# Output projection of a hybrid decoder layer: another order of its 32 products, split weight tiles shared between token quarters, and the MLP's first operands made in two rounds

## The chip, the cores and the metric

One core of one Trainium2 chip runs the whole layer in one launch. The metric is the device time of one execution in microseconds (us).

## The reference

One decoder layer, all in float32, for 2048 tokens of width 1024. The change touches the point where the two groups of mixer heads end and the MLP begins:

```python
mix = concatenate([gdn_out, hgrn_out])          # 2048 x 1024
y   = mix @ w_out                                # output projection, 1024 x 1024
h1  = x + rms_norm(y, post_mix_norm)             # norm over the 1024 columns of a token
t   = rms_norm(h1, pre_mlp_norm)
u   = relu(t @ w_mlp_up) ** 2                    # 1024 x 4096
m   = u @ w_mlp_down
```

Behind it the residual, a norm and a gated input embedding follow; they are not touched.

## The kernel before

**Layout.** Activations stand transposed: a tile is 128 features on the partitions by 512 tokens. The 2048 tokens are four quarters `q` of 512 (`NQ`), the 1024 features eight blocks of 128 (`KD`). A product of the projection, `mmo_q_d`, gives feature block `d` of quarter `q`; it accumulates over the eight blocks `k` of the mixed heads.

**Split operands.** A float32 operand is split into a high and a low part (`split`, L160 ff.): ACT copies it rounded (L164), DVE subtracts (L165). A product of two split operands takes three matmuls, so one `mmo` is 8 x 3 = 24 matmuls. A split weight tile of `w_out` (`whl`, 1 MB, three buffers) serves all k of one d. It is made from a raw tile of 512 KB (`raw`, two buffers, `stage_out`, load L338). `split_in_place` does the same to the mixed heads `mixT`, which `mix_operands(q)` loads (the tiles live in a ring of 28 buffers that also takes the MLP's operands).

**Order.** The 32 products run in the list `order`: all eight d of quarter 0, then 1, 2, 3. I call the places in this list slots, 0 to 31. Slots 0 and 1 are computed earlier, while the previous stage ends (`held`). At slot j the program makes the split tile of slot j + 2 ready (`ready_out`) and loads the raw tile of slot j + 3 (`stage_out`). Quarters 0, 1 and 2 load raw tiles and split them anew, 24 times; in quarter 0 the split tile is also stored to memory (`keep`, `cache_out`, 1 MB each), and quarter 3 reloads it from there (`reload`, L185).

**Agenda.** Work beside the products is written as generators. `later(gen, offsets)` sets their steps on a clock that ticks once in eight matmuls of PE (`mm`, `tick`); a step's instructions are then put into the queues at that place. Each engine, and SP as the queue for most DMAs, runs its instructions in that order.

- After each product: ACT copies the result out of PSUM (L1392, `yo`), ACT and DVE add its square to a sum (`squares`, L233 and L234). Quarters 2 and 3 store `yo` to memory (`yod`).
- Norm of a quarter after its last product (`rstd_steps`): the sum is split (`hl_o`), two matmuls with ones on PE spread it over partitions (`nrm_o`, L1174 and L1175), then ACT (Ln, Exp, Square) and DVE make the reciprocal root `r_o`.
- Quarters 0 and 1 go on in `normed`, `residual_by_dma`: for each d DVE scales `yo` (L1228), POOL issues a DMA that adds x from memory onto it (L1229); five steps later its square is added (`sq_h`, `acc_h`) and SP stores it as `h1d` (L1232). The sum of these squares is split (`hl_h`) and goes through PE as `nrm_h`, which gives the second norm's root `rn`. The steps stand in `OUT_STEPS`: 1 for `hl_o`, 5 for `nrm_o`, 7 to 19 for the residual, 20 for `hl_h`, 26 for `nrm_h`.
- Quarters 2 and 3 store a row of `r_o`; their residual comes later.
- MLP operands of the first half (quarters 0 and 1): the up product uses seven combinations of tiles per k (`11, 3, 1, 2, 21, 4, 22`). `early_operands` makes the ones that need quarter 0 alone (`11` and `21`: load `be`, multiply, split), from slot 17 on; `up_operands(0, ...)` the five others, `run(early)` first, from the slot after the second quarter's `nrm_h`, for each k all five in turn.
- In the last slots the raw tiles of the first up weights are loaded (`u_raw`) and split (`w_u`). Then the first MLP group runs (`u`, also L1143), with the fourth quarter's `nrm_o` among its matmuls.

Of the kernel before, what the change touches and what calls it, by code (L numbers as in the profile page):

```python
# [20 lines left out]
P = 128  # L21
# [22 lines left out]
N_CONST = C_MASK + len(LEVELS)  # L44


OUT_STEPS = (1, 5) + tuple(range(7, 20)) + (20, 26)
MLP_STEPS = (1, 5) + tuple(range(7, 25, 2))
AMID_STEPS = (1, 5) + tuple(range(12, 39, 3))

# [38 lines left out]
def trunk(ctx, tc, x, xT, pT, vecs, w_in, w_ab, gdn_a_log, gdn_dt_bias, w_out, w_up, w_down,  # L89
# [19 lines left out]
    def blk(c):  # L109
        return slice(c * P, (c + 1) * P)  # L110
# [51 lines left out]
    def split(t, eng, raw):  # L162

        S.activation(t[:, 0], raw, AF.Copy)  # L164
        eng.tensor_tensor(t[:, 1], raw, t[:, 0], ALU.subtract)  # L165
# [11 lines left out]
    def keep(key, w):  # L177

        c = dr.tile([P, 2 * KD * P], F32, name=f"cache_{key}")
        nc.sync.dma_start(c, w.bitcast(F32).rearrange("p h k n -> p (h k n)"))  # L180
        cached[key] = c

    def reload(key, name):
        w = wp.tile([P, 2, KD, P], F32R, tag="whl", name=f"w_{name}")
        nc.sync.dma_start(w.bitcast(F32).rearrange("p h k n -> p (h k n)"), cached[key])  # L185
        return w
# [142 lines left out]
            xin[q].append(t)  # L329
            yield  # L330

    order = [(q, d) for q in range(NQ) for d in range(KD)]
    staged_out, ready, RAW = {}, {}, 3

    def stage_out(j):
        if j < len(order) and order[j][0] < RAW:
            raw = wp.tile([P, KD, P], F32, tag="raw", name=f"raw_out{j}", bufs=2)
            nc.sync.dma_start(raw, w_out[order[j][1]])  # L338
            staged_out[j] = raw

    def ready_out(j):
        if j >= len(order):
            return
        if j not in staged_out:
            ready[j] = reload(f"out{order[j][1]}", f"out{j}")
            return
        ready[j] = wp.tile([P, 2, KD, P], F32R, tag="whl", name=f"w_out{j}")
        split(ready[j], V, staged_out.pop(j))
        if order[j][0] == 0:
            keep(f"out{order[j][1]}", ready[j])  # L350

    clock, agenda = [0], {}

# [927 lines left out]
    def early_operands():  # L1281

        start_operands(0)
        for k in range(KD // 2):
            for n, kk in (("11", k), ("21", k + KD // 2)):
# [3 lines left out]
                moving(0, n, k, b)  # L1289
                yield  # L1290

    def up_operands(half, rsb):

        qs = (2 * half, 2 * half + 1)
        early = half in tops
        if not early:
            start_operands(half)
        for k in range(KD // 2):
            n = f"{half}_{k}"
            b11, b21, b12, b22, t3, t2, t4 = (once(lambda i=i: ytile(f"b{i}_{n}")) for i in range(7))  # L1300
            if early:
                b11, b21 = (lambda k=k: first_b[k]), (lambda k=k: first_b[k + KD // 2])
            for b, s, kk in ((b12, 1, k), (b22, 1, k + KD // 2), (b11, 0, k), (b21, 0, k + KD // 2)):
                if early and s == 0:
                    continue
# [3 lines left out]
            if not early:  # L1309
                moving(half, "11", k, b11())  # L1310
# [8 lines left out]
            if not early:  # L1319
                moving(half, "21", k, b21())  # L1320
# [30 lines left out]
        return halves[1]  # L1351

    pair[0] = True
    for j, (q, d) in enumerate(order):
        if d == 0:
            ys, acc = [], None
            if q < 2:
                later(mix_operands(q + 1), range(2, 18, 2))
            if q == 1:
                later(mix_operands(3), range(17, 25))  # L1360
        ready_out(j + 2)
        stage_out(j + 3)
        if j == len(order) - 5:
            u_raw = [wp.tile([P, 2, QT], F32, tag="raw", name=f"u_raw{i}", bufs=2) for i in range(2)]
            a1, a2 = w_up[0], w_up[FF // P // 2]
            for t, i, src in ((u_raw[0], 0, a1[:, : KD // 2]), (u_raw[1], 1, a1[:, KD // 2 :]),
                              (u_raw[0], 1, a2[:, : KD // 2]), (u_raw[1], 0, a2[:, KD // 2 :])):
                nc.sync.dma_start(t[:, i].rearrange("p (k n) -> p k n", n=P), src)
        if j == len(order) - 2:
            two_blocks(("11", u_raw[0][:, 0]), ("12", u_raw[1][:, 1]))  # L1370
        if j == len(order) - 1:
            (a11, a21), (s1, s4) = ((t[:, 0], t[:, 1]) for t in u_raw)
            b22 = two_blocks(("22", s1), None)
            V.tensor_tensor(s1, s1, a21, ALU.add)
            V.tensor_tensor(a21, a11, a21, ALU.subtract)
            V.tensor_tensor(a11, s1, a11, ALU.subtract)
            V.tensor_tensor(s4, s4, a11, ALU.subtract)
            u_block("3", b22, a21)
        if (q, d) == (2, 1):
            early = early_operands()  # L1380
            later(early, range(0, 2 * KD, 2))
        if prep is None and h1_r[1] is not None:
            run(early)
            prep = up_operands(0, h1_r)
            later(prep, range(0, 24, 1))
        if j in held:
            ps = held.pop(j)
        else:
            ps = bank(f"mmo_{q}_{d}", pp)
            product(ps, columns(ready.pop(j)), xin[q])  # L1390
        y = ytile(f"yo{q}_{d}") if q < 2 else tp.tile([P, QT], F32, tag="stg", name=f"yo{q}_{d}")
        S.activation(y, ps, AF.Copy)  # L1392
# [439 lines left out]
```

## Time and profile before

| | us |
|---|---|
| three runs: median (lowest to highest) | 2725.19 (2724.35 to 2733.05) |
| profiled execution: span | 2719.9 |
| PE busy in it | 2660.8 (98%) |
| DVE busy | 2040.8 (75%) |
| ACT busy | 1464.0 (54%) |
| POOL busy | 118.5 (4%) |
| slots 2 to 31 of the projection | 1127.46 to 1313.90 |
| first MLP group | 1313.90 to 1335.43 |

The profiled execution has no time of its own beside its span; the span is 5.3 us under the median of the runs, and a change of the span is set against that median. PE's busy time says little about its rate, since matmuls overlap: a matmul's record lasts about 0.39 us, while in an undisturbed run one starts every 0.227 us. So the pitch, the gaps and the granted clock are what to look at. In the rows of the profile buffer numbers are left out: `w_out`, `yo`, `t` stand for all tiles of that name.

### The profile page before, as it was taken

The numbers are of one execution on the slowest core, as the hardware profiler recorded it, in microseconds if no ns is written. First come the engines' busy times: TensorE is split into PE (matmuls) and PEld (weight loads), VectorE is DVE, ScalarE is ACT, GpSimd is POOL, SyncE is SP. The second block draws the span as 40 slices with busy tenths as digits, with TensorE's granted clock in tenths as the row PEclk, the third lists the DMA queues.
The fourth block names the chain that finished last, engine by engine and source line by source line (L and its number), as shares of the span: only waits on it lengthen the run. The fifth ranks groups of instructions, "written<-read, shape, count | busy, mean of one in ns | idle before, by whom it ended". The sixth has DMA issues, their size and how long they took to land.

```text
span 2719.9 us, 38475 instructions
## 1 busy us (share of the span) xinstructions
PE 2660.8 (98%) x12745; PEld 2215.1 (81%) x12745; DVE 2040.8 (75%) x4219; ACT 1464.0 (54%) x2940; POOL 118.5 (4%) x133
## 2 busy tenths in 40 slices
PE   8999999999999999998999999999999999999999
PEld 6788888888888887876788888888888888888887
DVE  7778878787777777576989867768787765567776
ACT  7665555465445455575655646555555545465432
POOL 0000000000000000011000000001000000001000
PEclk9999999999999999998999999999999999999999
DMA  8777777667666665887566457667454346577663
GB/s 282 273 237 255 236 263 242 216 214 241 213 201 221 223 213 164 271 281 231 177 232 228 175 178 240 216 202 244 164 196 163 139 172 207 193 256 247 216 212 131
DMA packets 268742, 589.24 MB, mean 217 GB/s; under 512 B 55658, under 2 KB 60232, under 8 KB 249344
## 3 DMA queue, kind: packets, MB, share of 16 engines
q1 hardware_dynamic: 266240, 582.59, 63.9%
q0 software_dynamic: 2304, 4.20, 0.9%
q8 instruction: 101, 1.65, 0.3%
q14 instruction: 97, 0.79, 0.1%
HBM read 419.75 MB, written 166.92 MB: 216 GB/s over the span
## 4 chain that ended last, share of the span: by engine, by line
PE 51%; DMA 3%; DVE 3%; issue 3%; ACT 1%; POOL 1%; SPq 0%; POOLq 0%; DVEq 0%; ACTq 0%
PE d L1143 22%; PE u L1143 22%; PE mmg L1143 6%; PE mmo L1143 1%; DMA raw_out<-in_w_out_dram 1%; DMA yo<-in_xT_dram 0%; PE mme L191 0%; POOL acc_y L234 0%; DMA b<-h1d 0%; DMA w_out<-cache_out 0%; DMA db<-hid 0%; DVE t L165 0%; DMA h1d<-yo 0%; POOL yo L1229 0%; DVE pr_g L698 0%
## 5 line engine op out<-in xcount | busy, mean ns | idle before, releaser
L1072 PE MATMUL mm<-xt,w 128*128 128x512 f32 x3072 | 784.1, 400 | 1.4 <-ACT zt_zg L577 1.1
L1072 PEld LDWEIGHTS mm<-xt,w 128*128 128x128 f32 x3072 | 553.3, 189 | 102.3 <-ACT zt_zg L577 1.5
L1143 PE MATMUL d<-db,da 128*128 128x512 f32 x2688 | 611.0, 389 | 0.5 <-ACT db L217 0.2
L1143 PE MATMUL u<-t,wu 128*128 128x512 f32 x2604 | 591.1, 389 | 0.0
L1143 PEld LDWEIGHTS d<-db,da 128*128 128x128 f32 x2688 | 504.3, 188 | 106.4 <-DVE db L218 1.0
L1143 PEld LDWEIGHTS u<-t,wu 128*128 128x128 f32 x2604 | 488.7, 188 | 101.5
L218 DVE TENSOR_TENSOR db<-db 128x512 fp32r<-128x512 f32 x224 | 159.9, 714 | 72.4 <-ACT db L217 71.7
L1495 DVE TENSOR_TENSOR u<-u,u 128x512 f32<-128x512 f32 x224 | 150.2, 681 | 58.1 <-PE u L1143 56.6
L1143 PE MATMUL mmo<-mixT,w_out 128*128 128x512 f32 x720 | 173.4, 402 | 11.8 <-DMA w_out<-cache_out 5.5
L217 ACT ACTIVATE db<-db 128x512 fp32r<-128x512 f32 x224 | 140.9, 629 | 78.2 <-DMA db<-hid 71.9
L1143 PEld LDWEIGHTS mmo<-mixT,w_out 128*128 128x128 f32 x720 | 139.5, 195 | 44.6 <-DMA w_out<-cache_out 5.9
L1143 PE MATMUL mmg<-h2T,wg 128*128 128x512 f32 (+1 forms) x792 | 174.8, 383 | 0.0
L1538 ACT ACTIVATE u<-u 128x512 f32<-128x512 f32 x128 | 80.8, 631 | 166.3 <-DVE u L1495 166.0
L1143 PEld LDWEIGHTS mmg<-h2T,wg 128*128 128x128 f32 x792 | 145.5, 188 | 29.1
L165 DVE TENSOR_TENSOR da<-da 128x512 fp32r<-128x512 f32 x128 | 93.7, 732 | 77.7 <-ACT da L164 77.1
L164 ACT ACTIVATE da<-da 128x512 fp32r<-128x512 f32 x128 | 80.5, 629 | 124.8 <-DMA da<-sumd 91.6
L164 ACT ACTIVATE wu<-a 128x512 fp32r<-128x512 f32 x124 | 75.0, 623 | 44.3 <-DMA a<-in_w_up_dram 43.0
L698 DVE TENSOR_TENSOR pr_g<-xs_g,sys_g 128x16 f32<-128x16 f32 (+14 forms) x240 | 94.4, 393 | 5.6
L165 DVE TENSOR_TENSOR wu<-a,wu 128x512 fp32r<-128x512 f32 x124 | 85.6, 693 | 10.8 <-ACT wu L164 10.5
L234 POOL TENSOR_TENSOR acc_y<-acc_y,sq_y 128x512 f32<-128x512 f32 x28 | 38.5, 1374 | 1261.6 <-ACT sq_y L233 1260.8
L1539 ACT ACTIVATE u<-u 128x512 f32<-128x512 f32 x128 | 80.5, 629 | 3.1
L165 DVE TENSOR_TENSOR da<-dr,da 128x512 fp32r<-128x512 f32 x96 | 66.3, 691 | 19.0 <-ACT da L164 16.5
(385 smaller groups left out, 3792.6 us busy)
## 6 DMA issues: line engine op xcount, KB each, us to landing
w<-cache_in SPq DMA_DIRECT2D x96, 1024.0 KB
db<-hid SPq DMA_DIRECT2D x224, 256.0 KB
cache_in<-w SPq DMA_DIRECT2D x32, 1024.0 KB
hid<-u SPq DMA_DIRECT2D x128, 256.0 KB
da<-sumd SPq DMA_DIRECT2D x128, 256.0 KB
a<-in_w_up_dram SPq DMA_DIRECT2D x124, 256.0 KB
hid<-ht SPq DMA_DIRECT2D x96, 256.0 KB
dr<-in_w_down_dram SPq DMA_DIRECT2D x96, 256.0 KB
```

What stands on the lines that cost most here:

```text
L164: S.activation(t[:, 0], raw, AF.Copy)
L165: eng.tensor_tensor(t[:, 1], raw, t[:, 0], ALU.subtract)
L217: S.activation(t[:, 0], plain(t), AF.Copy)
L218: V.tensor_tensor(t[:, 1], plain(t), t[:, 0], ALU.subtract)
L234: eng.tensor_tensor(acc, acc, sq, ALU.add)
L698: V.tensor_tensor(pr[:, :, :, 0:i], xs[:, None, :, 0:i].broadcast_to([P, 2, GC, i]), sys[:, 0:i, i : i + 2].rearrange("p j two -> p two j" ...
L1072: PE.matmul(ps, *terms[i], start=i == 0, stop=i == nt - 1)
L1143: PE.matmul(ps, a, b, start=start, stop=stop)
L1495: V.tensor_tensor(c[new], c[old], ps, ALU.add)
L1538: S.activation(c[k], c[k], AF.Relu)
L1539: S.activation(c[k], c[k], AF.Square)
```

## The change

- `OUT_ORDER` lists the slots as quarter and block: quarter 0 as before, then quarter 1 from block 7 back, then quarters 2 and 3 mixed. A split tile stays for up to three slots that use the same block, if it is among those of the last six slots (`SHARE`). 19 tiles are loaded and split; none is stored or reloaded.
- `ready_at(n)`: tile n is split at the slot after the third last tile in use was used for the last time (three buffers); `stage_at(n)`: its raw tile is loaded one slot after tile n - 2 was split (two buffers). The order gives these slots (load: slot of the load, slot of the split, slots that use it):

```
 5: 2, 3: 5 10      6: 3, 4: 6 9       7: 4, 5: 7 8       8: 5, 9: 11
 9: 6,10: 12       10: 10,11: 13      11: 11,12: 14 16 18  12: 12,13: 15 17 20
13: 13,14: 19 22   14: 14,19: 21 24   15: 15,21: 23 25   16: 20,23: 26 29
17: 22,25: 27 30   18: 24,26: 28 31
```

- The mixed heads of all later quarters are set on the agenda at slot 0.
- The second quarter's steps are `OUT_LAST`: `nrm_o` at 4, residual from 5 to 17, `hl_h` at 19, `nrm_h` at 23.
- `rest_operands` replaces `up_operands` for the first half: round one makes tiles 3 and 4 of each k, round two tiles 2, 1 and 22 of each k from what round one kept. It starts at slot 24 (was 25).
- The third quarter's norm follows slot 28; the fourth's steps are 12, 20 and 24, so that its `nrm_o` falls into the second MLP group.

```diff
--- before.py
+++ after.py
@@ -44,7 +44,10 @@
 N_CONST = C_MASK + len(LEVELS)
 
 
+OUT_ORDER = ("00 01 02 03 04 05 06 07 17 16 15 12 13 14 10 11 20 21 30 22 31 23 32 24 33 34 25 26 27 35 36 37")
+SHARE = 6
 OUT_STEPS = (1, 5) + tuple(range(7, 20)) + (20, 26)
+OUT_LAST = (1, 4) + tuple(range(5, 18)) + (19, 23)
 MLP_STEPS = (1, 5) + tuple(range(7, 25, 2))
 AMID_STEPS = (1, 5) + tuple(range(12, 39, 3))
 
@@ -329,25 +332,31 @@
             xin[q].append(t)
             yield
 
-    order = [(q, d) for q in range(NQ) for d in range(KD)]
-    staged_out, ready, RAW = {}, {}, 3
-
-    def stage_out(j):
-        if j < len(order) and order[j][0] < RAW:
-            raw = wp.tile([P, KD, P], F32, tag="raw", name=f"raw_out{j}", bufs=2)
-            nc.sync.dma_start(raw, w_out[order[j][1]])
-            staged_out[j] = raw
-
-    def ready_out(j):
-        if j >= len(order):
-            return
-        if j not in staged_out:
-            ready[j] = reload(f"out{order[j][1]}", f"out{j}")
-            return
-        ready[j] = wp.tile([P, 2, KD, P], F32R, tag="whl", name=f"w_out{j}")
-        split(ready[j], V, staged_out.pop(j))
-        if order[j][0] == 0:
-            keep(f"out{order[j][1]}", ready[j])
+    order = [(int(s[0]), int(s[1])) for s in OUT_ORDER.split()]
+    load_of, last_use, tile_of = [], [], []
+    for j, (q, d) in enumerate(order):
+        recent = [n for n in range(len(tile_of)) if tile_of[n] == d and n in load_of[-SHARE:]]
+        if not recent:
+            recent = [len(tile_of)]
+            tile_of.append(d)
+            last_use.append(j)
+        load_of.append(recent[0])
+        last_use[recent[0]] = j
+    staged_out, ready = {}, {}
+
+    def ready_at(n):
+        return 0 if n < 3 else sorted(last_use[:n])[n - 3] + 1
+
+    def stage_at(n):
+        return 0 if n < 4 else ready_at(n - 2) + 1
+
+    def stage_out(n):
+        staged_out[n] = wp.tile([P, KD, P], F32, tag="raw", name=f"raw_out{n}", bufs=2)
+        nc.sync.dma_start(staged_out[n], w_out[tile_of[n]])
+
+    def ready_out(n):
+        ready[n] = wp.tile([P, 2, KD, P], F32R, tag="whl", name=f"w_out{n}")
+        split(ready[n], V, staged_out.pop(n))
 
     clock, agenda = [0], {}
 
@@ -1289,25 +1298,44 @@
                 moving(0, n, k, b)
                 yield
 
+    def rest_operands(rsb):
+
+        held = []
+        for k in range(KD // 2):
+            b11, b21 = first_b[k], first_b[k + KD // 2]
+            b12, b22 = ytile(f"b2_0_{k}"), ytile(f"b3_0_{k}")
+            for b, kk in ((b12, k), (b22, k + KD // 2)):
+                nc.sync.dma_start(b, h1d[1][kk])
+                V.scalar_tensor_tensor(b, b, col(R_PREMLP + kk), rsb, ALU.mult, ALU.mult)
+            yield
+            t3 = ytile(f"b4_0_{k}")
+            V.tensor_tensor(t3, b22, b12, ALU.subtract)
+            V.tensor_tensor(b12, b12, b11, ALU.subtract)
+            moving(0, "3", k, t3)
+            yield
+            t2, t4 = ytile(f"b5_0_{k}"), ytile(f"b6_0_{k}")
+            V.tensor_tensor(t2, b22, b12, ALU.subtract)
+            V.tensor_tensor(t4, b21, t2, ALU.subtract)
+            moving(0, "4", k, t4)
+            held.append((t2, b12, b22))
+            yield
+        for k, raws in enumerate(held):
+            for n, raw in zip(("2", "1", "22"), raws):
+                moving(0, n, k, raw)
+                yield
+
 ...
@@ -1351,15 +1378,19 @@
         return halves[1]
 
     pair[0] = True
+    early = None
+    made, square_sums = {q: [None] * KD for q in range(NQ)}, {q: None for q in range(NQ)}
     for j, (q, d) in enumerate(order):
-        if d == 0:
-            ys, acc = [], None
-            if q < 2:
-                later(mix_operands(q + 1), range(2, 18, 2))
-            if q == 1:
-                later(mix_operands(3), range(17, 25))
-        ready_out(j + 2)
-        stage_out(j + 3)
+        if j == 0:
+            later(mix_operands(1), range(2, 18, 2))
+            later(mix_operands(2), range(20, 36, 2))
+            later(mix_operands(3), range(35, 43))
+        for n in range(2, len(tile_of)):
+            if ready_at(n) == j:
+                ready_out(n)
+        for n in range(3, len(tile_of)):
+            if stage_at(n) == j:
+                stage_out(n)
         if j == len(order) - 5:
             u_raw = [wp.tile([P, 2, QT], F32, tag="raw", name=f"u_raw{i}", bufs=2) for i in range(2)]
             a1, a2 = w_up[0], w_up[FF // P // 2]
@@ -1376,28 +1407,31 @@
             V.tensor_tensor(a11, s1, a11, ALU.subtract)
             V.tensor_tensor(s4, s4, a11, ALU.subtract)
             u_block("3", b22, a21)
-        if (q, d) == (2, 1):
+            later(prep, range(3 * KD // 2))
+        if early is None and h1_r[0] is not None:
             early = early_operands()
             later(early, range(0, 2 * KD, 2))
         if prep is None and h1_r[1] is not None:
             run(early)
-            prep = up_operands(0, h1_r)
-            later(prep, range(0, 24, 1))
+            prep = rest_operands(h1_r[1])
+            later(prep, range(3 * KD // 2))
         if j in held:
             ps = held.pop(j)
         else:
             ps = bank(f"mmo_{q}_{d}", pp)
-            product(ps, columns(ready.pop(j)), xin[q])
+            product(ps, columns(ready[load_of[j]]), xin[q])
         y = ytile(f"yo{q}_{d}") if q < 2 else tp.tile([P, QT], F32, tag="stg", name=f"yo{q}_{d}")
         S.activation(y, ps, AF.Copy)
-        acc = squares(acc, ps, d, f"o{q}")
-        ys.append(y)
+        acc = square_sums[q] = squares(square_sums[q], ps, d, f"o{q}")
+        made[q][d] = y
         if q >= 2:
             nc.sync.dma_start(yod[q][d], y)
-        if d == KD - 1 and q < 2:
-            later(normed(q, ys, acc, lambda d, q=q: xT[blk(d), tok(q)], R_POSTMIX, h1d[q], "o", "h"), OUT_STEPS)
-        elif d == KD - 1:
-            later(rstd_steps(acc, 1.0 / D, EPS, f"o{q}", row_of(o_r, q), po, wait=True), OUT_STEPS[:2] + (9,))
+        if all(of != q for of, _ in order[j + 1 :]) and q < 2:
+            later(normed(q, made[q], acc, lambda d, q=q: xT[blk(d), tok(q)], R_POSTMIX, h1d[q], "o", "h"),
+                  OUT_LAST if q else OUT_STEPS)
+        elif all(of != q for of, _ in order[j + 1 :]):
+            later(rstd_steps(acc, 1.0 / D, EPS, f"o{q}", row_of(o_r, q), po, wait=True),
+                  OUT_STEPS[:2] + (9,) if q == 2 else (12, 20, 24))
     u_block("2", two_blocks(("1", s1), None), a11)
     u_block("4", wp.tile([P, 2, KD // 2, P], F32R, tag="raw", name="w_u4", bufs=2), s4)
     run(prep)
```

More of the change, by code (lines that the diff above doesn't have):

```diff
@@ L1290, in early_operands @@
                 yield
+    def rest_operands(rsb):
[22 more added lines that the diff above has]
+                yield
     def up_operands(half, rsb):
         qs = (2 * half, 2 * half + 1)
-        early = half in tops
-        if not early:
-            start_operands(half)
+        start_operands(half)
         for k in range(KD // 2):
@@ L1300, in up_operands @@
             b11, b21, b12, b22, t3, t2, t4 = (once(lambda i=i: ytile(f"b{i}_{n}")) for i in range(7))
-            if early:
-                b11, b21 = (lambda k=k: first_b[k]), (lambda k=k: first_b[k + KD // 2])
             for b, s, kk in ((b12, 1, k), (b22, 1, k + KD // 2), (b11, 0, k), (b21, 0, k + KD // 2)):
-                if early and s == 0:
-                    continue
                 nc.sync.dma_start(b(), h1d[qs[s]][kk])
@@ L1308, in up_operands @@
             yield
-            if not early:
-                moving(half, "11", k, b11())
+            moving(half, "11", k, b11())
             V.tensor_tensor(t3(), b22(), b12(), ALU.subtract)
@@ L1318, in up_operands @@
             moving(half, "2", k, t2())
-            if not early:
-                moving(half, "21", k, b21())
+            moving(half, "21", k, b21())
             yield
```

## Prediction

> **What bounds the kernel now.** TensorE is busy for almost the whole span, so the question is only where it is not at its pitch in the stage that the change rewrites: output projection and first group of the MLP's up product. I cut that stretch into windows. The columns are window and length, then busy time (instructions) of PE, PEld, DVE, ACT and POOL, the granted clock, the DMA share and GB/s; the first row is the whole stretch, the others are parts of it.
>
> ```profile
> 1127.46:1335.43 207.97, 195.07 (x817) 157.34 (x816) 144.44 (x215) 127.51 (x201) 16.33 (x18) 0.96 0.75 241
> 1127.46:1173.58 46.12, 43.75 (x186) 35.47 (x184) 22.48 (x30) 23.96 (x38) 2.01 (x2) 0.96 0.86 298
> 1232.49:1272.93 40.44, 31.57 (x110) 24.40 (x111) 25.55 (x38) 16.63 (x29) 7.07 (x8) 0.83 0.96 282
> 1272.93:1313.90 40.97, 40.97 (x182) 33.70 (x180) 33.15 (x53) 27.75 (x45) 0.00 (x0) 1.00 0.61 216
> 1313.90:1335.43 21.53, 20.39 (x87) 15.98 (x86) 18.85 (x32) 14.13 (x22) 0.00 (x0) 1.00 0.23 74
> ```
>
> Next the timeline of PE, for the undisturbed pitch and the waits (start, length, line, operation, count, in brackets idle time before it and what ended it).
>
> ```profile
> 1162.13 0.73 PE L1143 MATMUL mmo<-mixT,w_out 128*128 128x512 f32 x2 [1.85 <-ACT w_out L164]
> 1163.39 10.35 PE L1143 MATMUL mmo<-mixT,w_out 128*128 128x512 f32 x38 [0.53 <-DVE w_out L165]
> 1173.58 0.39 PE L1174 MATMUL nrm_o<-hl_o,ones 128*128 128x512 f32 x1
> 1173.80 0.39 PE L1175 MATMUL nrm_o<-hl_o,ones 128*128 128x512 f32 x1
> 1174.03 38.24 PE L1143 MATMUL mmo<-mixT,w_out 128*128 128x512 f32 x168
> 1212.11 0.39 PE L1174 MATMUL nrm_h<-hl_h,ones 128*128 128x512 f32 x1
> ...
> 1218.00 0.39 PE L1174 MATMUL nrm_o<-hl_o,ones 128*128 128x512 f32 x1
> ...
> 1266.44 6.65 PE L1143 MATMUL mmo<-mixT,w_out 128*128 128x512 f32 x16 [5.47 <-DMA w_out<-cache_out]
> 1272.93 0.39 PE L1174 MATMUL nrm_h<-hl_h,ones 128*128 128x512 f32 x1
> ```
>
> From 1174.03 to 1212.11 there are 168 matmuls without a wait: 38.08/168 = 0.2267 us each, 5.44 us for a tile of 24 (a "slot"; there are 32, numbered 0 to 31, the first two computed earlier). The whole stretch holds 816 matmuls (the row counts 817, one at a border): 816 x 0.2267 = 185.0. It took 207.97. **So 23.0 us can be won here at most.** The same sum for the parts: 46.12 - 184 x 0.2267 = 4.4 in the first window (slot 8), 40.44 - 110 x 0.2267 = 15.5 in the second (slots 23 and 24), 0 in the third to within the count, 21.53 - 86 x 0.2267 = 2.0 in the last (the MLP's first group); the remaining 1 us lies between.
>
> The waits alone are less than that: at slot 8 they are 1.85 + 0.53 = 2.38 us of the 4.4 lost. The clock explains the rest (window, PE busy, granted clock, DMA share, GB/s):
>
> ```profile
> 1162.00:1164.00 2.00, 1.34 (x4) 0.77 0.68 255
> 1164.00:1166.00 2.00, 2.00 (x6) 0.50 0.72 242
> 1166.00:1168.00 2.00, 2.00 (x9) 0.87 1.03 356
> 1266.00:1268.00 2.00, 1.56 (x4) 0.50 1.03 427
> 1268.00:1270.00 2.00, 2.00 (x6) 0.50 1.03 414
> ```
>
> After two waits of together 2.4 us the clock stands at half for about 3 us: 4.4 - 2.4 = 2.0 us extra for one stall.
>
> Who makes them? At slot 8, ACT: the split of the weight tile stands in its queue behind the copy of the previous slot's result. At slots 23 and 24, SP's queue:
>
> ```profile
> 1160.32 0.60 ACT L1392 ACTIVATE yo<-mmo 128x512 f32<-128x512 f32 x1 [3.13 <-PE mmo L1143]
> 1161.02 1.06 ACT L164 ACTIVATE w_out<-raw_out 128x1024 fp32r<-128x1024 f32 x1
> ```
>
> ```profile
> 1241.45 10.15 SPq L1232 DMA_DIRECT2D h1d<-yo  x4
> ...
> 1258.18 0.42 SPq L185 DMA_DIRECT2D w_out<-cache_out  x1
> ```
>
> SP is in order. Each store h1d<-yo waits for an accumulating DMA from POOL, so four of them hold SP for 10 us, and the first reload from the cache is issued at 1258.18 and awaited until 1266.44.
>
> **The change part by part.**
>
> *Shared split tiles, no cache.* Loads go from 24 raw tiles, 4 + 4 cache stores and 8 reloads to 19 raw tiles (the rows show the part inside the stretch):
>
> ```profile
> L165 DVE TENSOR_TENSOR w_out<-raw_out,w_out 128x1024 fp32r<-128x1024 f32 x20 | 24.4, 1221 | 18.5 <-ACT w_out L164 18.5
> L164 ACT ACTIVATE w_out<-raw_out 128x1024 fp32r<-128x1024 f32 x20 | 21.1, 1057 | 8.2 <-DMA raw_out<-in_w_out_dram 8.1
> ```
>
> ```profile
> raw_out<-in_w_out_dram SPq DMA_DIRECT2D x20, 512.0 KB
> w_out<-cache_out SPq DMA_DIRECT2D x8, 1024.0 KB
> ```
>
> 24 x 0.5 + 8 + 8 = 28 MB become 9.5 MB. Five splits fewer are 5 x 1.22 = 6.1 us of DVE and 5 x 1.06 = 5.3 us of ACT. I cost both at nothing by themselves: DVE is busy 144.4 of 208 us, DMA 0.75. What counts is when a tile is ready. In the new order slot 8 repeats column 7 with the tile of slot 7, so the split that was late there no longer exists: 4.4 us go. At slots 23 and 24 there is no reload: 15.5 go. The other splits are written at least two slots (10.9 us) before their first use; only the following are tight.
>
> *Slot 6.* Its split now stands on DVE behind the last head's gating, whose row comes back through a DMA. I take 0.3 us, between 0 and the 1.85 of slot 8.
>
> *The second quarter's norm, three ticks sooner (a tick is 8 matmuls, 1.81 us).* The chain goes from nrm_o through POOL's eight accumulating DMAs to hl_h, which nrm_h on PE needs; it now starts at tick 4 and ends at 23 (was 5 and 26). PE gives it 19 x 1.81 + 0.45 for a norm pair = 34.9 us. What it takes, from DVE's timeline and POOL's issues:
>
> ```profile
> 1209.99 0.68 DVE L165 TENSOR_TENSOR hl_h<-acc_h,hl_h 128x512 fp32r<-128x512 f32 x1
> ...
> 1261.66 0.69 DVE L165 TENSOR_TENSOR hl_h<-acc_h,hl_h 128x512 fp32r<-128x512 f32 x1 [0.70 <-ACT hl_h L164]
> ```
>
> ```profile
> 1185.46 2.02 POOL L1229 DMA_DIRECT2D yo<-in_xT_dram  x2 [42.08 <-DVE acc_o L234]
> ...
> 1235.53 0.87 POOL L1229 DMA_DIRECT2D yo<-in_xT_dram  x1 [40.24 <-DVE yo L1228]
> ```
>
> ```profile
> DMA to landing us min/median/max: 3.7/8.8/11.8
> ```
>
> In the first quarter 1210.67 - 1173.58 = 37.1 us; in the second 1262.35 - 1218.00 = 44.3. The first issue came 11.9 us after nrm_o in the first quarter and 17.5 in the second; from there to hl_h it took 25.2 and 26.8. In the second quarter DVE did other work ahead of the first scaling: four multiplications for the MLP's operands, four of their splits and two weight splits. In the changed kernel's order these are three, two and none. That is 0.7 + 2 x 0.7 + 2 x 1.22 = 4.5 us less, so the first issue comes after 13.0, and with the first quarter's 25.2 (DMA has less to move) the chain takes 38.2. PE waits 38.2 - 34.9 = 3.3 us in slot 23, partly for w_out's split (its hi half stands on ACT behind squares that wait for the accumulates), partly for hl_h. With a half clock as at slot 8, 2.0 more. The bounds: 0 if the chain fits, 9.4 + 2.0 if it is as slow as the second quarter was. Behind the waiting nrm_h on PE stand the last 8 matmuls of slot 23 and all later ones; DVE and ACT wait for those.
>
> The Trainium skill ("TensorE: Matmul & The Clock Gate", Part 1: The HAM clock gate) puts the fall to half rate after an idle window of about 3.4 us. By that rule 3.3 us in two pieces would cost no clock and the sum below would be 2.0 better. The trace disagrees: 2.38 us of waiting, in two pieces, gave 0.50.
>
> *MLP's first operands in two rounds, from one slot earlier.* The same 20 subtractions and splits, only ordered: tiles 3 and 4 first, then 2, 1 and 22. The ring of 28 buffers frees only as slots 28 and 31 pass, so some of the splits must run after slot 31. About 15 DVE operations are left then, at 0.6 to 0.7 us 9 to 10 us, against 21.5 us of that group, of which DVE worked 18.9 before. Cost 0 to 2.0 (what the group loses now); I take 1.0 for this and all other reordering together.
>
> *The last norm later.* nrm_o of the fourth quarter moves out of the first group into the second. Its two matmuls are executed all the same; what PE waited for them is part of the 2.0 above.
>
> **Sum:** -23.0 + 0.3 + 3.3 + 2.0 + 1.0 = -16.4. From about the third group on (the first ends at 1335.43), the order on every engine is the same. All of PE's waits behind that point are these (total, times, longest), so nothing takes the gain back there:
>
> ```profile
> PE nrm_y L1175 <- DVE hl_y L165: 0.6, 1, 0.6
> PE d L1143 <- ACT db L217: 0.2, 1, 0.2
> PE d L1143 <- DVE db L218: 0.2, 1, 0.2
> ```
>
> The profiled span is 2719.9, 5.3 under the median 2725.2: 2719.9 - 16.4 + 5.3 = 2708.8.
>
> **The rivals.**
>
> *No wait is left (chance 0.12).* The chain also gains from emptier queues and fits 34.9: -23 + 1.3 = -21.7, 2703.5. For it: the stretch moves a third less (18.5 of 208 x 0.241 = 50 MB). Against: the accumulates are issued one behind the other.
>
> *The waits stay, but without the clock (0.10).* 3.3 us fall in two pieces too short to halve the clock: -18.4, 2706.8. This is the mechanism of the skill's rule. Against it stands the 0.50 after 2.38 us.
>
> *The second quarter's chain is as slow as before (0.25).* Its 44.3 us meet 34.9: 9.4 + 2.0 at slot 23, with 0.3 and 1.0: -10.3, 2714.9. For it: operand tiles still stand among the scalings. With a second half clock and 5 us more of waiting it reaches 2722.
>
> *The accumulates hold SP and ACT again (slower, 0.10).* Raw tiles 16, 17 and 18 are issued on SP in slots 20, 22 and 24, in the very stretch of the h1d stores. Had each to wait as the reload did (5.5 and 2.0 for the clock), slots 26, 27 and 28 would lose 22.5; with 11.4 at slot 23 and 1.3, 35.2 are lost where 23.0 are won: +12, 2737. It decides when the last accumulate lands over some 45 us after nrm_o; before, the last store of the quarter was past 1258 - 1218 = 40. Against: each of these loads has two slots or more to spare, and there is less traffic.
>
> *The gain is given back or never comes (0.08).* DVE is near its limit at the end (33.15 of 40.97, 18.85 of 21.53), and three splits of 1.22 now fall there in place of reloads. A backlog of 18 us would show as PE's waits for t or w_u in the first group: 2719 to 2729.
>
> **How the numbers follow.** My forecast has 0.35, from 2705 to 2713. The range 2700 to 2722 takes in the first three cases beside it: 0.35 + 0.12 + 0.10 + 0.25 = 0.82. A difference of 0.3% is 8.2 us, about what a measurement of this kernel tells from none. Faster than 2717.0: 0.35 + 0.12 + 0.10 and 0.17 of the third, 0.74. Within: 0.08 of the third, 0.06 of the last, 0.02 of the slower one, 0.16. Slower: 0.08 + 0.02 = 0.10.
>
> **What would show it.** Right: no cache_out row, 19 raw_out loads, no wait at slot 8, one place with 1 to 5 us of waiting some 85 us after slot 8's old stall, the granted clock otherwise 1.0, and the stretch from 1127 to the second group's start about 190 us. Wrong: a wait at slots 26 to 28 for w_out, one for t in the first group, or new waits of PE before 1127 or after the first group.

## The result, and the profile after

| | median us (runs) | ratio to before | 95% interval |
|---|---|---|---|
| before | 2725.92 (9: 2718.84 to 2733.91) | | |
| changed | 2713.01 (9: 2708.69 to 2724.07) | 0.9955 | 0.994 to 0.9969 |

12.9 us faster, where 16.4 were forecast. The time lies in the stated range and the direction is the forecast one; not all terms of the sum held.

The profiled execution of the changed kernel is a long one: 2722.85 us (span 2721.1) against a median of 2713.01. Of that, 6.8 us are there before the two programs differ: the 5551st matmul, in the mixer stage, starts at 1072.7 instead of 1065.9 in the profile of before, and up to there the instructions are the same. So spans can't be compared here; stretches can. The windows of the changed kernel that answer to those of before (columns as there; first the whole stretch, then slots 2 to 9, 17 to 23, 23 to 31, first MLP group):

```profile
1139.16:1336.17 197.01, 189.76 (x816) 154.57 (x814) 136.57 (x204) 116.51 (x187) 18.28 (x18) 0.98 0.56 170
1139.16:1185.99 46.83, 43.86 (x186) 35.51 (x184) 26.88 (x39) 28.16 (x46) 3.92 (x2) 0.96 0.60 201
1229.05:1266.54 37.49, 35.76 (x156) 28.75 (x154) 29.31 (x45) 23.43 (x38) 7.07 (x8) 1.00 0.70 191
1266.54:1312.40 45.86, 45.86 (x203) 37.90 (x202) 36.74 (x55) 25.90 (x42) 0.00 (x0) 1.00 0.43 144
1312.40:1336.17 23.77, 21.22 (x86) 16.75 (x84) 18.41 (x31) 14.52 (x27) 0.00 (x0) 0.93 0.10 35
```

The stretch takes 197.0 instead of 208.0, DMA moves 170 instead of 241 GB/s. At the pitch of 0.2267 us, 12.4 us are still lost, at three places: 46.83 - 184 x 0.2267 = 5.1 around slot 6, 37.49 - 154 x 0.2267 = 2.6 in slot 23, 23.77 - 84 x 0.2267 = 4.7 in the first MLP group. PE's timeline has the waits:

```profile
1162.84 0.73 PE L1152 MATMUL mmo<-mixT,w_out 128*128 128x512 f32 x2 [1.76 <-ACT w_out L167]
1164.79 21.36 PE L1152 MATMUL mmo<-mixT,w_out 128*128 128x512 f32 x86 [1.21 <-DVE w_out L168]
...
1261.37 3.47 PE L1152 MATMUL mmo<-mixT,w_out 128*128 128x512 f32 x14 [0.88 <-DVE w_out L168]
1265.39 0.50 PE L1183 MATMUL nrm_h<-hl_h,ones 128*128 128x512 f32 x1 [0.55 <-ACT hl_h L167]
1266.20 0.50 PE L1184 MATMUL nrm_h<-hl_h,ones 128*128 128x512 f32 x1 [0.31 <-DVE hl_h L168]
...
1320.13 0.73 PE L1152 MATMUL u<-t,w_u 128*128 128x512 f32 x2 [2.13 <-ACT w_u L167]
1321.28 15.05 PE L1152 MATMUL u<-t,w_u 128*128 128x512 f32 x58 [0.41 <-DVE w_u L168]
```

Slot 8's old wait and the two long ones of slots 23 and 24 (2.25 for a split, 5.47 for a reload) are gone; three short ones remain in slot 23. The trace has 19 loads of `raw_out` and no row of `cache_out`, as forecast. The wait around slot 6 is new; here is ACT's timeline ahead of it:

```profile
1160.24 0.63 ACT L220 ACTIVATE mixT<-mixT 128x512 fp32r<-128x512 f32 x1 [4.99 <-DMA mixT<-mixd]
1160.78 0.58 ACT L1424 ACTIVATE yo<-mmo 128x512 f32<-128x512 f32 x1
1161.26 0.59 ACT L236 ACTIVATE sq_o<-mmo 128x512 f32<-128x512 f32 x1
1161.73 1.06 ACT L167 ACTIVATE w_out<-raw_out 128x1024 fp32r<-128x1024 f32 x1
```

ACT waited 5 us for a tile of mixT that is, by the program's order, the first of quarter 2 and needed in slot 16; the weight split that PE waits for stands behind it. In the kernel before, ACT split this tile at 1167.82, in slot 9, and did not wait for it. And one wait lies ahead of the stretch, in the mixer stage (DVE's row, then PE's):

```profile
1122.02 0.75 DVE L602 SCALAR_TENSOR_TENSOR og_g<-og_g,cols,rsb_g 128x512 f32<-128x512 f32 x1 [2.51 <-DMA rsb_g<-rd_g]
1122.69 0.34 DVE L775 SCALAR_TENSOR_TENSOR r_g<-vt_g,inv_g,psa_g 128x128 f32<-128x128 f32 x1
```

```profile
1123.09 0.49 PE L778 MATMUL psb_g<-r_g,xt_full 128*128 128x128 f32 x2 [2.46 <-DVE r_g L775]
```

A gating that waits for a row by DMA stands ahead of the small r_g that PE needs. In the kernel before, DVE had the two in the other order, and PE did not wait for r_g:

```profile
1111.33 0.35 DVE L766 SCALAR_TENSOR_TENSOR r_g<-vt_g,inv_g,psa_g 128x128 f32<-128x128 f32 x1
1112.64 0.75 DVE L593 SCALAR_TENSOR_TENSOR og_g<-og_g,cols,rsb_g 128x512 f32<-128x512 f32 x1 [0.96 <-DMA rsb_g<-rd_g]
```

### The profile page after: what moved, and what is told of

The parts are those of the page before. It is cut to its first block, busy times and chain, and to the rows that moved or that the text cites. A ratio compares the mean times of both kernels' runs of the same rounds, so it can differ in the third digit from the quotient of the medians.

```text
span 2721.1 us, 38423 instructions
## 1 busy us (share of the span) xinstructions
PE 2657.8 (98%) x12745; PEld 2211.9 (81%) x12745; DVE 2035.3 (75%) x4214; ACT 1459.7 (54%) x2935; POOL 121.1 (4%) x133
## 4 chain that ended last, share of the span: by engine, by line
PE 50%; DMA 4%; issue 3%; DVE 2%; ACT 1%; POOL 1%; SPq 0%; POOLq 0%; DVEq 0%; ACTq 0%
PE u L1152 22%; PE d L1152 21%; PE mmg L1152 6%; PE mmo L1152 1%; DMA mixT<-mixd 1%; POOL acc_y L237 1%; DMA yo<-in_xT_dram 0%; DMA h1d<-yo 0%; POOL yo L1238 0%; DMA rd_g<-m_g 0%; DMA raw_pT<-in_pT_dram 0%; ACT sq_y L236 0%; DMA rd_h<-m_h 0%; DMA raw_out<-in_w_out_dram 0%; DMA dr<-in_w_down_dram 0%
## 5 line engine op out<-in xcount | busy, mean ns | idle before, releaser
L1152 PE MATMUL mmo<-mixT,w_out 128*128 128x512 f32 x720 | 166.7, 392 | 3.8 <-DVE w_out L168 2.1
```

What stands on the lines that cost most here:

```text
L1152: PE.matmul(ps, a, b, start=start, stop=stop)
```

## The experiments

Two lengths are read from each trace, by counting PE's matmuls: the **mixer's end**, from the 5551st matmul to the first of slot 3, and the **stretch**, from there to the second MLP group. The first four expectations count the stretch from 1127.5 in the kernel before, which is the start of slot 2; their figures are 5.44 us larger than those of the table for the same thing. "Loses" means time over 5.44 us for a slot, or over 84 x 0.2267 for the MLP group, a pair of norm matmuls (0.45) taken off wherever it falls. Mixer's end and stretch come from one profiled execution of each kernel.

| kernel | median us (before, same chip) | ratio, 95% interval | mixer's end | stretch |
|---|---|---|---|---|
| before | 2725.92 | | 67.0 | 202.5 |
| before, again | 2720.61 (2723.47), one run | | 67.1 | 202.0 |
| changed | 2713.01 (2725.92) | 0.9955 (0.994 to 0.9969) | 71.9 | 191.6 |
| changed, again | 2710.66 (2723.47) | 0.995 (0.9935 to 0.9965) | 68.5 | 188.5 |
| before, raw tiles to slot 27 | 2721.61 (2723.47) | 0.9994 (0.9985 to 1.0003) | 68.2 | 197.0 |
| mixT behind weights | 2707.27 (2723.47) | 0.994 (0.9923 to 0.9957) | 66.7 | 184.7 |
| order and sharing alone | 2717.93 (2720.88) | 0.9985 (0.9975 to 0.9994) | 68.5 | 194.5 |
| old steps, second quarter | 2712.45 (2720.88), one run | | 69.9 | 187.1 |
| one round | 2725.34 (2720.88), one run | | 72.2 | 197.4 |
| old steps, fourth quarter | 2718.2 (2720.88), one run | | 68.0 | 196.9 |
| + slots exchanged | 2708.78 (2722.13) | 0.9946 (0.9932 to 0.9961) | 71.2 | 185.7 |
| + third quarter's norm later | 2704.3 (2722.13) | 0.9929 (0.9912 to 0.9945) | 70.0 | 183.2 |
| + old steps, second quarter | 2705.01 (2721.6) | 0.9936 (0.9925 to 0.9948) | 70.8 | 183.1 |
| + og_g behind r_g | 2696.27 (2716.3) | 0.9929 (0.9915 to 0.9943) | 66.6 | 183.0 |

**The same two kernels again.** No edit.

> The kernel before, profiled once more, for the scatter between executions. The stretch from the first mmo of slot 3 to the second MLP group took 207.97 us in the first profile and began at 1127.5. First theory (the early part of the program scatters from run to run, the stretch does not): beginning within 7 us of 1127, stretch 206 to 210, the same three places of waiting. Rival (the waits themselves are accidents of one execution): the waits at slots 8, 23 and 24 come out differently by more than 5 us.

Mixer's end and stretch came out within 0.5 us of the first profile (207.5 from slot 2). The waits at slots 23 and 24 changed their lengths but not their sum; PE's timeline:

```profile
1250.99 5.30 PE L1143 MATMUL mmo<-mixT,w_out 128*128 128x512 f32 x22 [2.09 <-DVE w_out L165]
1265.24 6.24 PE L1143 MATMUL mmo<-mixT,w_out 128*128 128x512 f32 x16 [8.95 <-DMA w_out<-cache_out]
```

The reload's wait was 8.95 instead of 5.47, and these slots lost 14.0 us against 13.7. Slots 7 and 8 lost 2.8 instead of 4.4: the waits were nearly the same (1.63 + 0.53 us), but the granted clock stayed at 1.00 there. So the first theory held for the whole stretch, while a single wait scatters by 3.5 us, and the half clock is not sure to follow a wait.

> The changed kernel, profiled once more. In its first profile the stretch began at 1139.2 (11.7 later than before) and took 197.0. First theory (the late beginning is mostly scatter of the execution, since the medians differ by 12.9 and the profiles by nothing): it begins at 1125 to 1134, the stretch takes 195 to 199, time 12 us under before. Rival (the change itself delays the end of the mixer stage by 5 to 12 us, by the other order of DVE and ACT there): it begins at 1136 to 1142 again.

Time again 12.8 us under before (2710.66 to 2723.47). The stretch took 194.0 from slot 2, 1 us under what was expected: 4.6 lost at slot 6, 2.3 in slot 23, 2.6 in the MLP group. Slot 2 began at 1133.0, as the first theory had it. Against before that is 5.5 us late: 3.9 were there at the 5551st matmul, as scatter, and 1.6 come from a longer mixer's end. In the first profile these were 6.8 and 4.9. So most of the late beginning is scatter ahead of the change; the rest lies in the mixer's end. This execution (2712.55 us) is near the median, and its mixer's end and stretch together are 12.5 us shorter than before (257.0 against 269.5), about the measured gain.

**mixT's splits behind the weight splits.** (The names newest[0] and [1] are the latest weight split on ACT and DVE; the edges order the queues and add no wait.)

```diff
-            split_in_place(t)
+            if q and newest:
+                with tc.issue_after(newest[0].ins), tc.issue_after(newest[1].ins):
+                    split_in_place(t)
...
+        newest[:] = [a, v]
```

> The changed kernel, in which no split of mixT on ACT and DVE may be put ahead of a weight split that the program wrote earlier. First theory (slot 6 loses 5.1 us because the list scheduler, with the cache stores gone, moved the mixT splits and their waits for DMA ahead of the weight split on ACT): PE's wait for w_out in slot 6 goes, the stretch takes 192 to 193 instead of 197. Rival (slot 6's split is late because of its raw tile or DVE's gating): the wait stays within 1 us of 3, the stretch is 196 to 198.

PE's timeline has no wait from the end of the mixers on:

```profile
1130.07 41.87 PE L1160 MATMUL mmo<-mixT,w_out 128*128 128x512 f32 x184
```

184 matmuls in 41.70 us, 0.2266 each. Slot 6's loss of 4.6 to 5.1 is gone, as the first theory said, and it stays away in the four kernels below that keep this edit: the place of the mixT splits is shown to be the cause. The stretch took 190.1 from slot 2, 2 us less than expected, since the expectation was set against the longer of the two profiles of after; against both, it is 3.8 to 6.9 shorter.

**The old order without early reloads.** Slots 24 to 27 get raw tiles, reloads come from slot 28 on.

```diff
-        if j < len(order) and order[j][0] < RAW:
+        if j < 28:
...
-        if order[j][0] == 0:
+        if order[j][0] == 0 and order[j][1] >= 4:
```

> The kernel before in its old order, with slots 24 to 27 served by raw tiles and fresh splits as the slots ahead, and reloads only from slot 28 on (four stores and four reloads fewer, 8 MB, four raw tiles more, 2 MB). First theory (what cost 15.5 us was the reload's place on SP behind the h1d stores, and shared tiles are not needed to win it): slots 23 and 24 lose under 5 us, the stretch takes 195 to 199, time some 10 us under before. Rival (the gain comes from the smaller traffic, which falls by 6 of 50 MB here against 18.5 in the change): the stretch takes 203 to 208.

Between the two: 202.4 from slot 2 (197.0 in the table). The 4.4 us of slots 7 and 8 are gone, which the edit was not aimed at, and slots 14 to 16 lose 2.7 anew. Slots 23 and 24 still lose 10.4 us. PE, then SP, then ACT:

```profile
1255.30 5.99 PE L1143 MATMUL mmo<-mixT,w_out 128*128 128x512 f32 x24 [2.25 <-DVE w_out L165]
1262.93 3.47 PE L1143 MATMUL mmo<-mixT,w_out 128*128 128x512 f32 x14 [1.65 <-DVE w_out L165]
1269.55 0.51 PE L1174 MATMUL nrm_h<-hl_h,ones 128*128 128x512 f32 x1 [3.15 <-ACT hl_h L164]
```

```profile
1254.09 4.96 SPq L1232 DMA_DIRECT2D h1d<-yo  x3
1259.10 3.44 SPq L1306 DMA_DIRECT2D b<-h1d  x2
1262.64 0.37 SPq L338 DMA_DIRECT2D raw_out<-in_w_out_dram  x1
```

```profile
1267.44 1.06 ACT L164 ACTIVATE w_out<-raw_out 128x1024 fp32r<-128x1024 f32 x1 [4.90 <-DMA raw_out<-in_w_out_dram]
```

A raw tile (for slot 25) is held on SP by the h1d stores, and by loads of what they stored, just as the reload was; ACT then waits 4.90 for it, and hl_h stands behind it on ACT. So my first theory was wrong in its main part: of the 13.7 to 14.0 us only some 3.5 go with the reload, and most stays when a raw tile has to be fetched while the accumulates land. The 2.25 of slot 23 is there with both and is no matter of SP: ACT had the raw tile, but split it behind a square that had waited 3.51 for an accumulate (4.73 in the kernel before), and DVE's half stood behind an operand split that ACT did later still. In the new order slots 21 to 25 use tiles whose loads went out in slots 13 to 15; that this is why it wins there is argued from the order and not tested by itself. With ratio 0.9994 the time shows no gain. This kernel shows one thing more: with four stores fewer, but in the old order, the scheduler already put the splits of quarter 1's mixT sooner (the first in slot 1 instead of 4) and the gating ahead of r_g, where PE waited 1.5. So both appear with fewer stores and do not need the new order.

**Parts of the change undone.** The new order with shared tiles, everything else as before:

```diff
...
-            prep = rest_operands(h1_r[1])
-            later(prep, range(3 * KD // 2))
+            prep = up_operands(0, h1_r)
+            later(prep, range(0, 24, 1))
...
-                  OUT_LAST if q else OUT_STEPS)
+                  OUT_STEPS)
...
-                  OUT_STEPS[:2] + (9,) if q == 2 else (12, 20, 24))
+                  OUT_STEPS[:2] + (9,))
```

> The new order and the shared tiles alone: the second quarter's norm, the MLP operands (one round, five tiles for each k) and the fourth quarter's norm as in the kernel before. The stretch from slot 3 to the second MLP group took 202.5 and 202.0 before, 191.6 and 188.5 after. First theory (all of the gain is the shared tiles; the three moved steps are worth nothing in sum): 188 to 192. Rival (the moved steps carry a part, since without them the operands come late for the first MLP group): 193 to 198, with the loss of the first MLP group at 6 or more instead of 2.6 to 4.7.

The rival's numbers: 194.5, and the MLP group loses 6.0. But PE waits for a weight split and not for operands:

```profile
PE u L1152 <- ACT w_u L167: 3.9, 1, 3.9
```

In time this kernel is only 3.0 us under before on its chip (2717.93 to 2720.88; interval 0.9975 to 0.9994), against 12.9 and 12.8 for the whole change, and the intervals do not overlap. So by the times most of the gain comes only with the moved steps. The profiles put less on them (194.5 against 188.5 and 191.6), and where the rest lies stays open; the profiled execution here was the longest of its ten (2722.93).

Each moved step alone undone (the third, second and first hunk above):

> The changed kernel with the fourth quarter's norm at its old steps, so that its two matmuls come in the first MLP group again. First theory: the two waits for hl_o of before (0.2 + 0.6) come back, the first group's loss rises by 0.5 to 1.5. Rival (ACT's queue is the limit there): it rises by 3 or more, as the norm's Ln and Exp with their table loads (1.28 each) stand ahead of weight splits.

The rival's size, but another cause: the MLP group lost 9.0 us, 4.12 of it in a wait for hl_o. ACT had made its half of hl_o by 1313.42; the other half stood on DVE behind operand splits that DVE worked off without a gap:

```profile
1315.12 3.10 DVE L168 TENSOR_TENSOR t<-b,t 128x512 fp32r<-128x512 f32 x5
1318.13 0.69 DVE L168 TENSOR_TENSOR hl_o<-acc_o,hl_o 128x512 fp32r<-128x512 f32 x1
```

> The changed kernel with the second quarter's norm at its old steps (5, 7 to 19, 20, 26). First theory (what PE waits for in slot 23 is mostly w_out's split behind squares that wait for the accumulates, so the norm's place costs little): the waits for hl_h (0.5 + 0.3) go, slot 23 and 24 lose 1 to 3 instead of 2.7 to 3.1. Rival (the norm sooner is what lets the MLP operands be ready): the first MLP group's loss rises from 2.6 to 4.7 to over 6.

The waits for hl_h went, but slots 22 and 23 lost 4.6 us, where 1 to 3 were expected, by waits of 1.84 and 0.53 for a weight split. The MLP group lost 2.0. The stretch, 187.1, is no longer than the changed kernel's, though slot 6 lost only 1.5 in this profile, some 3 less than there. No gain from moving this norm is shown.

> The changed kernel with the first MLP operands in one round again (for each k all five tiles in turn). First theory (the first group waits for its weight splits w_u and not for operands, so the rounds matter little): loss of the first group 2 to 5 as with two rounds. Rival (the ring is full until slots 28 and 31 pass, and one round blocks ACT and DVE on it): waits for t in the first group, or slots 29 to 31 lose, 5 us or more together.

Neither as written: the MLP group lost 10.0, but PE waited for a weight split and not for operands. PE's wait, and what stood on ACT ahead of that split, which ends at 1321.29:

```profile
PE u L1152 <- ACT w_u L167: 6.8, 1, 6.8
```

```profile
1317.49 0.60 ACT L236 ACTIVATE sq_o<-mmo 128x512 f32<-128x512 f32 x1 [0.98 <-DVE r_o L1193]
1317.99 1.14 ACT L167 ACTIVATE wu<-a 128x512 fp32r<-128x512 f32 x2
1319.45 0.63 ACT L167 ACTIVATE w_u<-u_raw 128x512 fp32r<-128x512 f32 x1 [0.33 <-DVE u_raw L1413]
1319.99 0.61 ACT L167 ACTIVATE hl_o<-acc_o 128x512 fp32r<-128x512 f32 x1
1320.66 0.63 ACT L167 ACTIVATE w_u<-u_raw 128x512 fp32r<-128x512 f32 x1
```

Here ACT waits for DVE in turn, which was busy without a gap from 1310.41 on. The new order makes quarters 2 and 3 end almost together, so two norms, the last squares, the operand splits and the weight splits meet on ACT and DVE. Two rounds and the later last norm pay for this cost of the order: together some 3 to 6 us of stretch (194.5 against 188.5 and 191.6). Undone singly they cost 5.3 to 8.9 us each, in one profile each; their effects do not add.

**Slots 23 and 24 exchanged**, on top of the ordered mixT splits:

```diff
-... 31 23 32 24 33 34 25 ...
+... 31 23 32 33 24 34 25 ...
```

> The changed kernel with mixT's splits kept behind the weight splits, and slots 23 and 24 exchanged (33 ahead of 24), so that the tile that is split in slot 21 is first needed one slot later. First theory (in slot 23 PE waits for that split, which stands on ACT behind squares that wait for the accumulating DMAs, and one slot is enough): the wait for w_out (1.5) goes, slots 23 and 24 lose 1 to 2.5 together instead of 3.8, the stretch takes 182 to 184 instead of 184.7. Rival (hl_h is as late as the split, and with the split's wait gone PE waits for hl_h as long): still 3.5 or more, the wait for hl_h at 2 instead of 0.9.

The wait for w_out went, and hl_h's grew (PE's timeline):

```profile
1255.08 0.49 PE L1191 MATMUL nrm_h<-hl_h,ones 128*128 128x512 f32 x1 [1.43 <-ACT hl_h L167]
```

Nearer to the rival: slot 23 lost 2.3 instead of 3.4, and the chain of accumulates is the limit there. The stretch is not shorter (185.7 against 184.7), since the MLP group lost 4.3 instead of 2.1.

**The third quarter's norm nine ticks later**, on top of that:

```diff
-                  OUT_STEPS[:2] + (9,) if q == 2 else (12, 20, 24))
+                  (10, 14, 18) if q == 2 else (12, 20, 24))
```

> The same, with the third quarter's norm nine ticks later (steps 10, 14, 18 instead of 1, 5, 9), behind slot 31. First theory (in the first MLP group PE waits for w_u because the Ln and Exp of that norm, with their two table loads of 1.28, hold ACT just there): the waits for w_u (1.1 + 0.4) go, the first group loses under 1 instead of 2.1. Rival (the norm only moves to a place as tight, ahead of other weight splits): the loss stays at 2 or grows, with a wait for hl_o or w_u.

The waits for w_u are gone and the MLP group loses nothing instead of 4.3, as the first theory had it. Slot 23 lost 4.1 instead of 2.3, at a half clock (last section). In the changed kernel that norm's table loads and Ln and Exp stood on ACT ahead of the weight splits:

```profile
1310.04 1.28 ACT L1188 ACT_TABLE_LOAD   x1
1311.80 0.63 ACT L1188 ACTIVATE r_o<-acc_o 128x512 f32<-128x512 f32 x1 [0.47 <-DVE acc_o L1187]
...
1316.29 3.22 ACT L167 ACTIVATE t<-b 128x512 fp32r<-128x512 f32 x6
1319.45 0.63 ACT L167 ACTIVATE w_u<-u_raw 128x512 fp32r<-128x512 f32 x1
```

**The second quarter's norm at its old steps**, on top of that.

```diff
-                  OUT_LAST if q else OUT_STEPS)
+                  OUT_STEPS)
```

> The changed kernel with four edits: mixT's splits kept behind the weight splits, slots 23 and 24 exchanged, the third quarter's norm nine ticks later, and the second quarter's norm back at its old steps (20 and 26 for hl_h and nrm_h). First theory (the last wait of PE in the stretch is nrm_h, planned three ticks sooner than the chain of accumulates can be; without it nothing is late): no wait over 0.5 in the stretch, which takes 179 to 181 instead of 183.2; time 2698 to 2703, some 20 us under before. Rival (the operands, begun one slot later, now come late for the first MLP group, which lost little only because the norm was soon): the first group loses 2 to 5, the stretch takes 183 to 186, time as before this edit or longer.

Stretch and time are the rival's (183.1 us, and a ratio of 0.9936 after 0.9929), but not by its cause: the MLP group loses nothing. Nor is the first theory right, since nrm_h, though three ticks later, still waits (1.60 + 0.22):

```profile
1260.11 0.50 PE L1191 MATMUL nrm_h<-hl_h,ones 128*128 128x512 f32 x1 [1.60 <-ACT hl_h L167]
```

From nrm_o at 1219.81 this took 40.3 us, in the changed kernel 36.8. The chain is made of the agenda's steps as well as of DMAs; with later steps it ends later. What would shorten it stays open.

**og_g behind r_g**, without the last edit:

```diff
...
+                tc.add_manual_dep(behind["og"].ins, behind["r"].ins.name, ...)
...
```

> The kernel with mixT's splits behind the weight splits, slots 23 and 24 exchanged and the third quarter's norm later (the second quarter's at the changed kernel's steps), and in the end of the mixer stage one more order held on DVE: the gating og_g of the last but one head, which waits for a DMA, behind r_g of the last head's third chunk, as it stood in the kernel before. First theory (the 2.0 to 2.5 us that PE waits there for r_g, in every kernel with the new weight loads and in none of the two profiles of before, come from this exchange in the scheduler's order): that wait goes, and the time from the last common instruction to slot 3 falls from 70.0 to 67 to 68. Rival (the wait is only shifted, since the same chain waits for the row by DMA a little later): a wait of PE of 2 or more appears in the next chunk or for hl_g, and the time stays at 69 to 71.

As the first theory had it, no wait for r_g is left; the mixer's end takes 66.6, a little under what was expected. But this length scatters by itself: the kernel with mixT behind weights took 66.7 with the exchange still in it and 1.4 us of waiting for r_g. So the cause of the wait is shown, and what it costs is not. PE's waits in the stretch are down to hl_h:

```profile
PE nrm_h L1205 <- ACT hl_h L167: 1.4, 1, 1.4
PE nrm_h L1206 <- DVE hl_h L168: 0.3, 1, 0.3
```

This kernel has the lowest median: 20.0 us under before on the same chip (2696.27 to 2716.3), against 12.9 and 12.8 for the change alone. But its ratio, 0.9929, is also that of the kernel without this edit: the times show no gain from it.

## Why the prediction was right, and where its sum was off

- **What is lost now (23.0):** right, and so were its places. 13.7 and 14.0 us at slots 23 and 24 in the two profiles of before, 4.4 and 2.8 at slots 7 and 8.
- **Slots 8, 23 and 24 won back (4.4 + 15.5):** these waits are gone, as forecast. Why a weight is late there I had put down to SP's queue and the reload. The old order with raw tiles still loses 10.4 there: SP's queue holds a raw tile too, the split of slot 23 stands on ACT behind squares that wait for accumulates, and the reload itself accounts for some 3.5 us.
- **Who wins the 23.0 (the order and the tiles; the moved steps only cost):** not as forecast. Order and tiles alone gain 3.0 us of time and lose 6.0 in the first MLP group; the 12.9 needs the moved steps beside them.
- **Slot 6 (0.3):** wrong; 5.1 and 4.6. I had seen that its DVE half waits behind the gating and had not asked what 18.5 MB less of DMA do to the scheduler: it now puts mixT's loads sooner, and their splits, with waits of some 5 us for DMA, on ACT ahead of the weight split. The edges that hold the order took this loss away. That the missing stores are what moved the splits is supported by the old order with four stores fewer, and not tested further.
- **The second quarter's norm (3.3 + 2.0 for the clock):** the chain was well sized: first issue 11.7 us after nrm_o (13.0 forecast), 37.6 to the end of hl_h (38.2), 2.6 and 2.3 lost, of which 1.74 and 1.42 in waits (3.3). The clock's 2.0 did not come: it stayed at 1.00. That was luck, since in three of the later kernels it halved at the wait for hl_h (below).
- **Operands, rounds, last norm (1.0):** mis-sized: 4.7 and 2.6, of which 2.5 and 2.0 in waits. I looked at DVE's backlog behind slot 31; in the changed kernel it was ACT (DVE's backlog shows when the last norm is put back). The third quarter now ends in slot 28 instead of 23, and its norm falls on ACT where the weights are split. I had left this out of the list of moved work altogether.
- **Nothing ahead of slot 2 (0):** wrong, and by the prediction's own list: new waits of PE before 1127 were one of its signs of being wrong. PE waits 2.5 and 2.3 us for r_g, by the exchange of og_g and r_g on DVE; the last experiment takes this wait away. The mixer's end is 1.6 to 4.9 us longer; how much of that is the exchange and how much scatter is not shown.
- **Sum:** 6.6 us were to remain in the stretch, 12.4 and 9.4 did, and the mixer's end adds to it. The errors that cost (slot 6, the MLP group, the mixer's end) and the one that gave (slot 23) cancel in part; that 12.9 came as near to 16.4 as it did is partly luck.
- **The rivals:** the second quarter's slow chain and a return of the waits at slots 26 to 28 did not come. Nothing was given back after the first MLP group: from its end to the last matmul 1379.7 and 1379.0 us before, 1380.2 and 1379.2 after. The clock's rival was right at slot 23 in both profiles, wrong at slot 6 in both, and right in the MLP group in one of the two: see the last section.

## What to carry to other kernels

When traffic or splits are taken away, list what the scheduler can now do sooner, and ask behind which DMA wait it puts the work that the bounding engine needs; on an in-order engine, early is harmful where it waits. A stretch is priced on every engine that a moved product drags along, its norm and its table loads on ACT too. A weight that is needed while stores on the same queue wait for other transfers must have been issued before them.

## What the runs showed of the hardware

Short waits halve the clock, but not always. The clock in windows of 2 us (window, busy PE, clock, DMA share, GB/s), first in the changed kernel after 0.88, 0.55 and 0.31 us of waiting, then in its second profile after 1.60 and 0.41 in the MLP group, then in the kernel with the third quarter's norm moved after 1.69 and 0.32, and in the one with og_g behind r_g after 1.42 and 0.30:

```profile
1264.00:1266.00 2.00, 1.34 (x5) 1.00 1.04 384
1266.00:1268.00 2.00, 1.80 (x8) 1.00 0.55 218
```

```profile
1312.00:1314.00 2.00, 1.09 (x4) 1.00 0.16 48
1314.00:1316.00 2.00, 2.00 (x10) 1.00 0.27 95
```

```profile
1250.00:1252.00 2.00, 0.77 (x2) 0.90 1.04 361
1252.00:1254.00 2.00, 2.00 (x5) 0.50 0.61 238
```

```profile
1246.00:1248.00 2.00, 1.42 (x5) 1.00 0.68 269
1248.00:1250.00 2.00, 2.00 (x7) 0.55 0.36 134
```

Two pieces of together 2.01 us halved it once and once not; 1.72 in two pieces did, 1.74 in three pieces did not. At slot 8 of the kernel before it was 1.85 + 0.53 in the first profile, with the half clock, and 1.63 + 0.53 in the second, without; of the 1.6 us between the losses (4.4 and 2.8) 0.2 is waiting, so some 1.4 goes with the clock, where the prediction had put 2.0. No length of waiting parts the two outcomes in these runs. The Trainium skill ("TensorE: Matmul & The Clock Gate", Part 1: The HAM clock gate) says that activity is judged in a free-running window, so that the same kernel can meet it differently. These rows fit that; its figure of about 3.4 us of idling before the clock falls is too long for them, as 1.72 us sufficed.
